# Product 3 of the first FFN's tiles a tile later, second buffers, and four banks for the transposes

## The chip, the cores and the metric

The kernel runs on one NeuronCore of a Trainium2 chip. The metric is the device time of one launch in microseconds (us). The engines have short names in the profile: PE is TensorE (matmuls and transposes; PEld its weight loads), DVE is VectorE, ACT is ScalarE, POOL is GpSimd, SP is SyncE, from whose queue most DMAs are issued. A lower time is better; the median of three runs is given, and one more execution was profiled.

## The reference

One layer of an encoder, applied with the same weights to a prompt of 1024 tokens and to a sample of 256 tokens, D = 1024, all in float32:

```
x <- LN1(alpha*x + 0.5*SwiGLU_1(x))
x <- LN2(alpha*x + W_out[ RMS(S5(x)) ; RMS(Hyena(x)) ])
x <- LN3(alpha*x + 0.5*SwiGLU_2(x))

_swiglu(x, w_gate, w_up, w_down) = (silu(x @ w_gate) * (x @ w_up)) @ w_down
```

The inner width of both FFNs is 2816, which is 22 tiles of 128. S5 is a bank of complex state space filters, Hyena a pair of long convolutions done with Fourier transforms. The change touches the first step of the prompt, above all; a detail of it touches the last.

## The kernel before

Float32 matmuls are made of three matmuls of a rounded format: each operand is split into a rounded part hi and a remainder lo, and hi times hi, hi times lo and lo times hi are added up in PSUM. `split` does this: ACT rounds (L171), DVE subtracts (L172).

The prompt's first FFN is done in two pieces. Two of its eight token tiles run with the sample's (`ffn`, L298 and L331 in the profile). The other six run in `ffn1_halves`: the token tiles are paired, and gate and up of a pair with the two halves of D are a product of 2 by 2 blocks, done with seven products instead of eight. `Blocks` makes the seven token operands: 11, 21 and 22 are blocks of the tokens, t1 to t4 their differences (on POOL, L1311). Each block of 128 by 512 is turned by four PE transposes into one PSUM bank (`Blocks.put`, L1318) and split from there. `GateUp` makes the seven weight operands of a tile of 128 inner columns: g1, g2 and u2 are blocks of the weights, s1 to s4 sums, which in the first FFN stand on POOL (L1373). Raw weights come by two DMAs of 512 KB per tile (L1345). The operand buffers of a weight are given back as soon as its product has been issued, so the next tile's split waits for that product on PE.

Product n of tile ft is written P(n, ft) below. Each is 12 matmuls of 128 by 384. Two sets of three PSUM banks alternate between tiles: bank a takes P1 and P2, bank b takes P6, P7 and P4, bank c takes P5 and P3, each adding on what is there. Between them the bank is read: after P1 a copy c1 (ACT), after P2 the first Silu (ACT L1437), after P6 the sum u2, after P7 two sums u3 (from b, then from c), after P4 the sum c1 and the product L1460, after P3 the sum, a second Silu (L1467) and the product L1468 (all sums are L1419 on DVE). The finished pair of h goes to DRAM by an SP DMA of 384 KB (L1488). After the last tile, `Down` reads it back and does the second matmul (L1552).

The order on PE in the loop of `gated` is: P1 of tile ft+1, P4 and P3 of ft, then P6, P5, P2 and P7 of ft+1. P4 has to wait until the first u3 sum has read bank b. u2 and u3 are the two halves of one buffer, and there is one buffer for h.

`weave` mixes two generators: while one issues the seven products, the other, `s5_mats`, prepares tables for S5 (cmul L424 to L429, L548 on DVE; a few matmuls; DMAs of scr_tab and scr_mat), by the shares that their yields name. The order of issue is turned into an order on each engine by a scheduler that goes by priority and estimated times.

Before the loop, `begin` issues the second pair of weight sums and the blocks 22 and t1 to t4 of all pairs (`Blocks.odd`). In the first FFN the transposes use banks 6 and 7 in turn, the last two that the products leave free.

The second FFN (prompt of eight token tiles, 128 by 512 matmuls) calls the same `gated`, with its weight sums on DVE, and with nothing woven in. Its first operands are made in `HyenaSide.prompt` while the mixer's last matmuls run, also through two banks.

Of the kernel before, what the change touches and what calls it, by code (L numbers as in the profile page):

```python
# [17 lines left out]
NFT = DFF // 128  # L18
# [10 lines left out]
PIECE = 2048  # L29
# [4 lines left out]
def prod(t):  # L34
    r = 1
    for v in t:
        r *= v
    return r


def shaped(ap, dims):
    if len(dims) == 1:
        return ap
    names = "abcde"[:len(dims)]
    return ap.rearrange("p (" + " ".join(names) + ") -> p " + " ".join(names), **dict(zip(names[1:], dims[1:])))
# [47 lines left out]
class Ring:  # L93
# [3 lines left out]
    def get(self):  # L97
        self.i += 1
        return self.bufs[(self.i - 1) % len(self.bufs)].v

    def free(self):
        for b in self.bufs:
            b.free()


class Banks:
# [436 lines left out]
def s5_mats(K, A, keep, scr, cfg):  # L543


    nc = K.nc
# [3 lines left out]
    turn, bs = K.new(7, 2, 32), K.new(2, 64, 16)  # L550
# [4 lines left out]
    for j in range(0, 32, 8):  # L555
        d, q = divmod(j, 16)
        c, s, t = c_.get(), s_.get(), tm.get()
        V.memset(c[:, :, 0:1], 1.0)
        V.memset(s[:, :, 0:1], 0.0)
        for lev in range(7):  # L560
            n = 1 << lev
# [16 lines left out]
    banks, bank1 = Banks(K, cfg["prep"][:-1]), Banks(K, cfg["prep"][-1:])  # L578
    bb, bb1 = bs.v[:, 0], bs.v[:, 1]
    pwr, pwi = K.pw[:, 0], K.pw[:, 1]  # L580
    cin, cst, gw = K.ring(2, 2, 2, 64), K.ring(1, 2, 8, 16), K.ring(2, 15, 16)
    inj, injt = K.ring(1, 4, 8, 16), K.ring(2, 4, 128)
    outm, tmp = K.ring(1, 4, 9, 16), K.ring(1, 4, 9, 16)
    nc.sync.dma_start(out=K.dcol, in_=g("ssm_d").rearrange("(b g) h -> (g h) b", b=4))
    for b in range(4):
        gv = gw.get()
# [58 lines left out]
        for s in range(8):  # L645
            nc.sync.dma_start(out=scr["mat"][s * 16:s * 16 + 16, b * 8:b * 8 + 8, 4].rearrange("h g x -> g h x"),
                              in_=gv[:, 7 - s:15 - s].rearrange("p t h -> p (t h)"))
    for r in (cin, cst, gw, inj, injt, outm, tmp, bs):
        r.free()


# [756 lines left out]
        self.w.pop(ft)  # L1408


def gated(K, X, G, hd, ids, begin, spare):

    nc = K.nc
    V = nc.vector
    T = X.width
    cr, tmp, hb = K.ring(2, T), K.new(2, T), K.ring(1, 2, T)
    TT = lambda o, a, b: V.tensor_tensor(out=o, in0=a, in1=b, op=ALU.add)  # L1419
    st = {}  # L1420
    END = NFT - 1

    def product(ft, n, bank, first):
        G.product(ft, n, X, st[ft]["ps"][bank], first)
        if ft == END:
            spare(n)

    def p1(ft):
        st[ft] = s = {"ps": [K.ps[:, b * 512:b * 512 + T] for b in ids[ft % 2]], "c1": cr.get()}
        product(ft, 1, 0, True)  # L1430
        nc.scalar.copy(out=s["c1"], in_=s["ps"][0])

    def p2(ft):
        s = st[ft]
        product(ft, 2, 0, False)
        s["h"] = hb.get()
        nc.scalar.activation(out=s["h"][:, 0], in_=s["ps"][0], func=AF.Silu)  # L1437

    def p6(ft):
        s = st[ft]  # L1440
        product(ft, 6, 1, True)
        s["u2"] = tmp.v[:, 0]
        TT(s["u2"], s["ps"][1], s["c1"])

    def p5(ft):
        product(ft, 5, 2, True)

    def p7(ft):
        s = st[ft]
        product(ft, 7, 1, False)  # L1450
        s["u3"] = tmp.v[:, 1]
        TT(s["u3"], s["ps"][1], s["c1"])
        TT(s["u3"], s["ps"][2], s["u3"])

    def p4(ft):
        s = st[ft]
        product(ft, 4, 1, False)
        h = s["h"][:, 0]
        TT(s["c1"], s["ps"][1], s["c1"])
        V.scalar_tensor_tensor(out=h, in0=s["c1"], scalar=0.5, in1=h, op0=ALU.mult, op1=ALU.mult)  # L1460

    def p3(ft):
        s = st[ft]
        product(ft, 3, 2, False)
        h = s["h"][:, 1]
        TT(h, s["ps"][2], s["u2"])
        nc.scalar.activation(out=h, in_=h, func=AF.Silu)  # L1467
        V.scalar_tensor_tensor(out=h, in0=s["u3"], scalar=0.5, in1=h, op0=ALU.mult, op1=ALU.mult)  # L1468

    p1(0)  # L1470
    p2(0)
    begin()
    G.parts(1)
    p1(1)
    p6(0)
    G.sums(1, 0)
    p5(0)
    G.sums(1, 1)
    p7(0)
    yield 0.6  # L1480
    for ft in range(NFT):
        if 0 < ft < END:
            p1(ft + 1)
        p4(ft)
        p3(ft)
        G.free(ft)
        G.load()
        nc.sync.dma_start(out=hd[ft], in_=st.pop(ft)["h"].rearrange("p a t -> p (a t)"))  # L1488
        yield 0.4
        if ft < END:  # L1490
            more = ft + 2 < NFT
            p6(ft + 1)
            if more:
                G.parts(ft + 2)
            p5(ft + 1)
            if more:
                G.sums(ft + 2, 0)
            p2(ft + 1)
            if more:
                G.sums(ft + 2, 1)  # L1500
            p7(ft + 1)
            yield 0.6
    for r in [cr, tmp, hb] + G.sv:
        r.free()


# [66 lines left out]
def run_all(gen):  # L1573
    for _ in gen:
        pass
# [18 lines left out]
def emit(ctx, tc, nc, A, dbg=None):  # L1594
# [34 lines left out]
    def tokens(ap, nm):  # L1629
        return ap.rearrange("(c s) d -> c s d", s=PARTS[nm][1])  # L1630
# [44 lines left out]

    def ffn1_halves(N, first, tail, turn):

        tb, src = Banks(K, (6, 7)), tokens(A["x_prompt"][0], "prompt")
        X = Blocks(K, N // 2, False)
        X.make(X.NAMES[0:2])  # L1680
        xs = [K.new(2, D) for _ in range(N // 2)]
        for j, x in enumerate(xs):
            for i in range(2):
                nc.sync.dma_start(out=x.v[:, i], in_=src[:, first + 2 * j + i])
            X.even(x.v, j, tb)
        G = GateUp(K, g("ffn1_w_gate"), g("ffn1_w_up"), True)
        G.load()
        yield 0.01
        G.parts(0)
        X.make(X.NAMES[2:])  # L1690
        G.load()

        def begin():
            G.sums(0, 0)
            G.sums(0, 1)
            for j, x in enumerate(xs):
                X.odd(x.v, j, tb)
                x.free()

        dn = Down(K, g("ffn1_w_down"), scr["h1"], N)  # L1700
        xr = []

        def spare(n):

            X.free(GateUp.OPS[n][1])
            if n in (1, 2):
                dn.load()
            elif n == 6:
                xr.append(Parts(K, N, D))
                for s in range(N):  # L1710
                    nc.sync.dma_start(out=xr[0].at(s), in_=src[:, first + s])

        yield from gated(K, X, G, scr["h1"], ((0, 1, 2), (3, 4, 5)), begin, spare)

        def done(s):
            nc.sync.dma_start(out=scr["x1_prompt"][:, first + s], in_=xr[0].at(s))
            turn(xr[0], s)

        yield from dn.run(xr[0], g("ln1_g"), g("ln1_b"), range(6), done, tail=tail)
        xr[0].free()  # L1720
# [65 lines left out]
    class HyenaSide:  # L1786


        def __init__(self, nm):
            self.nm, self.T = nm, NTOK[nm]  # L1790
            self.W = out_weights(K, A, 1)
# [37 lines left out]
        def prompt(self, ids, ids2, G):  # L1829


            tb = Banks(K, ids)
            self.norms(ids)
            lnb = self.norm_rows()
            x, nxt = {}, 0

            def load():
                nonlocal nxt
                x[nxt] = b = K.new(2, D)
                for i in range(2):  # L1840
                    nc.sync.dma_start(out=b.v[:, i], in_=scr["x1_prompt"][:, 2 * nxt + i])
                nxt += 1

            load()
            load()
            X = None

            def turn(j):
                X.even(x[j].v, j, tb)
                X.odd(x[j].v, j, tb)  # L1850
                x.pop(j).free()

            for j in range(4):
                for i in range(2):
                    s = 2 * j + i
                    for _ in mix_out(K, (s,), lambda s: x[j].v[:, i], self.hy, self.W, rs["prompt"][:, 1], ids2, lambda s: 0, 2):
                        pass
                    layer_norm(K, x[j].v[:, i], lnb.v[:, 0], lnb.v[:, 1], LN_EPS / ALPHA ** 2)
                    nc.sync.dma_start(out=scr["x2"][:, s], in_=x[j].v[:, i])
                    if i == 0 and j:  # L1860
                        if X is None:
                            X = Blocks(K, 4, True)
                            X.make(X.NAMES)
                        turn(j - 1)
                        if nxt < 4:
                            load()
                        elif j == 3:
                            G.load()
                free_all([self.hy[j]])
            free_all([self.W])  # L1870
            X.even(x[3].v, 3, tb)

            def begin():
                X.odd(x[3].v, 3, tb)
                x.pop(3).free()
                lnb.free()
                X.tmp.free()

            return X, begin
# [55 lines left out]
            for s in range(8):  # L1935
                nc.sync.dma_start(out=xr[0].at(s), in_=scr["x2"][:, s])

    run_all(gated(K, X, G, scr["h"], ((0, 1, 2), (3, 4, 5)), begin, spare))
    dst = tokens(A["out_prompt"], "prompt")

    def cut(c):
# [35 lines left out]
```

## Time and profile before

| what | us |
|---|---|
| median of three runs (lowest to highest) | 2590.32 (2585.53 to 2593.26) |
| the profiled execution | 2594.09 |
| its span, first to last instruction | 2592.3 |
| first FFN's products begin, six token tiles | 532.8 |
| first wait of the loop's P4 in PE's timeline | 571.7 |
| end of the first FFN's gate and up, about | 922 |
| second FFN's gate and up, about | 1915 to 2346 |
| its Down, to the end | 2346 to 2592 |

The mean granted clock of TensorE is 0.987 of the full one over the span. A row of a timeline has the start, the duration, the engine, the line, the operation, what is written from what (buffer numbers left out), shapes, a count of like instructions in a row, and in brackets the idle time of the engine ahead of it with what ended it. A row of the waits has the total, the number and the longest. A row of a window has the busy time of every engine, then PE's clock and the DMAs.

### The profile page before, as it was taken

How to read it: one execution, taken by the hardware profiler on the slowest of the kernel's cores; microseconds unless marked ns; L12 is line 12 of the kernel's file. 1: busy time of each engine (PE TensorE's matmuls, PEld its weight loads, DVE VectorE, ACT ScalarE, POOL GpSimd, SP SyncE). 2: the span in 40 equal slices, each digit the busy share in tenths (PEclk: the TensorE clock that was granted, in tenths of full speed). 3: DMA queues.
4: the chain of work that ended last, by engine and by line, in shares of the span. 5: the costliest groups of instructions: out<-in, count | busy, mean ns of one | idle time of the engine just before them, and what ended most of it. 6: DMA issues, size and time to landing. Idle time of an engine off the chain costs nothing.

```text
span 2592.3 us, 32411 instructions
## 1 busy us (share of the span) xinstructions
PE 2494.5 (96%) x12605; PEld 2123.9 (82%) x12605; DVE 1900.4 (73%) x2873; ACT 870.3 (34%) x1291; POOL 213.2 (8%) x158
## 2 busy tenths in 40 slices
PE   8999999988999999999999999999989999999998
PEld 6777777878899988888888878998768888888887
DVE  6887777697777886567896888788986656557437
ACT  5434443333333332223444313333332222223200
POOL 0000000143333300010000000000230000000001
PEclk9999999999999999999999999999989999999999
DMA  7333222434454564455565754565332322245311
GB/s 189 122 119 98 94 89 86 154 107 129 135 139 131 150 220 152 116 162 142 172 191 166 230 196 149 161 189 159 134 119 89 94 73 92 79 138 195 123 41 65
DMA packets 358704, 349.42 MB, mean 135 GB/s; under 512 B 41260, under 2 KB 308421, under 8 KB 357526
## 3 DMA queue, kind: packets, MB, share of 16 engines
q1 hardware_dynamic: 323510, 328.99, 40.5%
q10 hardware_dynamic: 35040, 18.35, 2.7%
q8 instruction: 99, 1.62, 0.3%
q14 instruction: 55, 0.45, 0.1%
HBM read 262.64 MB, written 84.39 MB: 134 GB/s over the span
## 4 chain that ended last, share of the span: by engine, by line
PE 69%; DVE 17%; DMA 5%; issue 3%; ACT 2%; POOL 2%; SPq 1%; ACTq 0%; DVEq 0%; POOLq 0%
PE banks L1398 24%; PE banks L1552 14%; PE banks L298 9%; PE banks L331 5%; DVE s L172 4%; PE banks L866 3%; DVE s L936 3%; PE banks L783 3%; PE banks L1248 2%; PE banks L1070 2%; ACT s L171 2%; POOL s L1373 1%; DVE s L751 1%; DMA s<-in_ffn_w_up_dram 1%; DMA s<-in_ffn_w_gate_dram 1%
## 5 line engine op out<-in xcount | busy, mean ns | idle before, releaser
L1398 PE MATMUL banks<-s,s 128*128 128x512 f32 (+1 forms) x3536 | 767.5, 369 | 19.4 <-DVE s L1419 15.6
L171 ACT ACTIVATE s<-s 128x1024 fp32r<-128x1024 f32 (+4 forms) x533 | 481.0, 916 | 855.6 <-PE banks L1398 176.0
L1398 PEld LDWEIGHTS banks<-s,s 128*128 128x128 f32 x3536 | 651.7, 191 | 97.6 <-DVE s L1419 15.6
L172 DVE TENSOR_TENSOR s<-s,s 128x1024 fp32r<-128x1024 f32 (+4 forms) x533 | 575.1, 1089 | 198.6 <-ACT s L171 187.0
L298 PE MATMUL banks<-s,s 128*128 128x512 f32 (+1 forms) x2112 | 400.9, 342 | 2.6 <-ACT s L171 1.7
L1552 PE MATMUL banks<-s,s 128*128 128x512 f32 x1232 | 386.8, 394 | 0.0
L298 PEld LDWEIGHTS banks<-s,s 128*128 128x128 f32 x2112 | 324.8, 191 | 53.6 <-issue 9.2
L1552 PEld LDWEIGHTS banks<-s,s 128*128 128x128 f32 x1232 | 230.4, 188 | 47.8 <-DVE s L172 0.4
L1552 PE MATMUL banks<-s 128*128 128x512 f32 x616 | 242.4, 394 | 0.0
L1419 DVE TENSOR_TENSOR s<-banks,s 128x384 f32<-128x384 f32 (+1 forms) x220 | 136.6, 621 | 139.0 <-PE banks L1398 137.5
L866 PE MATMUL banks<-s,s 128*128 128x512 f32 (+1 forms) x1152 | 237.6, 360 | 0.0
L866 PEld LDWEIGHTS banks<-s,s 128*128 128x128 f32 x1152 | 188.0, 189 | 28.0 <-DVE s L172 0.4
L331 PE MATMUL banks<-s,s 128*128 128x512 f32 x792 | 199.7, 398 | 3.0 <-DVE s L172 1.1
L1558 DVE TENSOR_TENSOR s<-banks,s 128x512 f32<-128x512 f32 x140 | 96.1, 688 | 129.4 <-PE banks L1552 129.4
L230 POOL TENSOR_TENSOR cst<-cst 128x1 f32<-128x1 f32 (+2 forms) x38 | 47.8, 1259 | 1619.5 <-DVE cst L229 1619.5
L331 PEld LDWEIGHTS banks<-s,s 128*128 128x128 f32 x792 | 146.7, 190 | 35.2 <-issue 1.9
L1552 PEld LDWEIGHTS banks<-s 128*128 128x128 f32 x616 | 115.8, 188 | 24.1
L1248 PE MATMUL banks<-s,s 128*128 128x512 f32 x480 | 124.3, 406 | 3.8 <-DVE s L1170 1.6
L1248 PEld LDWEIGHTS banks<-s,s 128*128 128x128 f32 x480 | 89.3, 191 | 23.4 <-DVE s L1170 2.0
L685 DVE TENSOR_TENSOR s<-banks,s 128x512 f32<-128x512 f32 (+2 forms) x112 | 58.8, 551 | 41.7 <-ACT s L802 20.8
L783 PEld LDWEIGHTS banks<-s,s 128*128 128x128 f32 x624 | 81.0, 190 | 7.1 <-ACT s L171 2.5
L783 PE MATMUL banks<-s,s 128*128 128x256 f32 x624 | 85.8, 285 | 0.0
(217 smaller groups left out, 2531.7 us busy)
## 6 DMA issues: line engine op xcount, KB each, us to landing
s<-in_ffn_w_gate_dram SPq DMA_DIRECT2D x88, 512.0 KB
s<-in_ffn_w_up_dram SPq DMA_DIRECT2D x88, 512.0 KB
s<-in_ffn_w_down_dram SPq DMA_DIRECT2D x88, 512.0 KB
scr_h<-s SPq DMA_DIRECT2D x22, 512.0 KB
s<-scr_h SPq DMA_DIRECT2D x22, 512.0 KB
scr_tab<-s ACTq DMA_DIRECT2D x32, 320.0 KB
s<-scr_mat SPq DMA_DIRECT2D x16, 640.0 KB
s<-scr_tab SPq DMA_DIRECT2D x16, 640.0 KB
```

What stands on the lines that cost most here:

```text
L171: K.nc.scalar.activation(out=hi, in_=src, func=AF.Copy)
L172: K.nc.vector.tensor_tensor(out=lo, in0=src, in1=hi.bitcast(F32), op=ALU.subtract)
L298: nc.tensor.matmul(pss[-1][c], lhsT=w[:, wv, d], rhs=xT.parts[k][c].at(d), start=(d == 0 and wv == 0 and k == 0), stop=(d == 7 and wv == 1))
L331: nc.tensor.matmul(ps, lhsT=h[s // 4][:, a, s % 4 * 128:(s % 4 + 1) * 128], rhs=w[:, b, dh * 512:(dh + 1) * 512], start=(n == 0), stop=(n ...
L783: nc.tensor.matmul(ps, lhsT=F[kt][a].v[:, s, i], rhs=b.v[:, s], start=(n == 0), stop=(n == 3 * NT // R - 1))
L866: nc.tensor.matmul(p, lhsT=w[:, wv, d], rhs=xT[nm].parts[k][c].at(d), start=(d == 0 and wv == 0 and k == 0), stop=(d == 7 and wv == 1))
L936: TT = lambda o, a, b, op: V.tensor_tensor(out=o, in0=a, in1=b, op=op)
L1248: nc.tensor.matmul(ps, lhsT=y[s // per][a].v[:, k, ts], rhs=W[k].v[:, b, dh * 512:dh * 512 + 512], start=(k == 0 and a == 0 and b == 0), s ...
L1398: self.K.nc.tensor.matmul(ps, lhsT=w[i][:, d], rhs=x[k][:, d], start=first and m == 0, stop=m == len(todo) - 1, skip_group_check=True)
L1419: TT = lambda o, a, b: V.tensor_tensor(out=o, in0=a, in1=b, op=ALU.add)
L1552: nc.tensor.matmul(ps, lhsT=p[a].v[:, o:o + 128], rhs=p[b].v[:, dh * 512:dh * 512 + 512], start=m == 0, stop=m == len(todo) - 1)
L1558: nc.vector.tensor_tensor(out=xv, in0=ps, in1=xv, op=ALU.add)
```

## The change

`gated` gets an argument `late`. Where it is true (first FFN), P3 of a tile is issued after P7 of the next one instead of behind P4 of its own; u2, u3 and h have two buffers each; the write of h to DRAM goes with P3; and the raw weights of a further tile are requested once a tile's sums are issued, after two more in `begin`, which puts them a tile further ahead. Where it is false (second FFN) the order of products stays. The transposes in `ffn1_halves` go through banks 4, 5, 6 and 7; those of the second FFN's operands through 2, 3 and two more, and in its `begin` through 4 to 7. The small rings of the S5 preparation are packed into two pieces of SBUF, and the buffers of `gated` are taken when first used.

The counts of instructions on PE, DVE, ACT and POOL stay the same.

```diff
+class Later(Ring):
+    def __init__(self, K, n, *dims):
+        super().__init__([])
+        self.K, self.n, self.dims = K, n, dims
+    def get(self):
+        if len(self.bufs) < self.n:
+            self.bufs.append(self.K.new(*self.dims))
+            self.i = len(self.bufs) - 1
+        return super().get()
...
-    cin, cst, gw = K.ring(2, 2, 2, 64), K.ring(1, 2, 8, 16), K.ring(2, 15, 16)
-    inj, injt = K.ring(1, 4, 8, 16), K.ring(2, 4, 128)
-    outm, tmp = K.ring(1, 4, 9, 16), K.ring(1, 4, 9, 16)
+    inj, injt, cin, whole1 = packed(K, (1, 4, 8, 16), (2, 4, 128), (2, 2, 2, 64))
+    outm, tmp, cst, gw, whole2 = packed(K, (1, 4, 9, 16), (1, 4, 9, 16), (1, 2, 8, 16), (2, 15, 16))
...
-def gated(K, X, G, hd, ids, begin, spare):
+def gated(K, X, G, hd, ids, begin, spare, late):
...
-    cr, tmp, hb = K.ring(2, T), K.new(2, T), K.ring(1, 2, T)
+    rings = cr, u2r, u3r, hb = [Later(K, n, *d) for n, *d in ((2, T), (1 + late, T), (1 + late, T), (1 + late, 2, T))]
...
         V.scalar_tensor_tensor(out=h, in0=s["u3"], scalar=0.5, in1=h, op0=ALU.mult, op1=ALU.mult)
+        G.free(ft)
+        nc.sync.dma_start(out=hd[ft], in_=st.pop(ft)["h"].rearrange("p a t -> p (a t)"))
+
+    def weights(ft, step):
+        if ft < NFT:
+            (G.parts, lambda f: G.sums(f, 0), lambda f: G.sums(f, 1))[step](ft)
+            if step == 2 and late:
+                G.load()
...
-    yield 0.6
+    yield 0.7
     for ft in range(NFT):
+        if ft and late:
+            p3(ft - 1)
         if 0 < ft < END:
             p1(ft + 1)
         p4(ft)
-        p3(ft)
-        G.free(ft)
-        G.load()
-        nc.sync.dma_start(out=hd[ft], in_=st.pop(ft)["h"].rearrange("p a t -> p (a t)"))
+        if not late:
+            p3(ft)
+            G.load()
         yield 0.4
         if ft < END:
...
             p6(ft + 1)
-            if more:
-                G.parts(ft + 2)
+            weights(ft + 2, 0)
             p5(ft + 1)
...
+            weights(ft + 2, 1)
             p2(ft + 1)
...
+            weights(ft + 2, 2)
             p7(ft + 1)
...
+    if late:
+        p3(END)
...
-        tb, src = Banks(K, (6, 7)), tokens(A["x_prompt"][0], "prompt")
+        tb, src = Banks(K, (4, 5, 6, 7)), tokens(A["x_prompt"][0], "prompt")
...
-        G.load()
 
         def begin():
             G.sums(0, 0)
             G.sums(0, 1)
+            G.load()
+            G.load()
...
-            tb = Banks(K, ids)
+            tb, tb2 = Banks(K, (2, 3) + ids), Banks(K, ids2 + ids)
...
-                X.odd(x[3].v, 3, tb)
+                X.odd(x[3].v, 3, tb2)
```

What this does to the engines shows in the middle of the first FFN's loop. First PE, where P7 of tile 9 ends (weights s_60 and s_61). Before, P1 of tile 10 (weights s_45 and s_46) follows, and after that P4 of tile 9:

```order
L1398 MATMUL banks<-s_61_3649,s_86_4913 128x384
L1398 MATMUL banks<-s_60_3648,s_86_4913 128x384
L1398 MATMUL banks<-s_45_3447 128x384
L1398 MATMUL banks<-s_46_3448,s_45_3447 128x384
L1398 MATMUL banks<-s_45_3447,s_46_3448 128x384
```

Now P3 of tile 8 (weights s_54 and s_55) stands there, with P1 of tile 10 and P4 of tile 9 behind it (L1426 is the L1398 of before):

```order
L1426 MATMUL banks<-s_61_3649,s_82_4749 128x384
L1426 MATMUL banks<-s_60_3648,s_82_4749 128x384
L1426 MATMUL banks<-s_54_3642,s_56_3644 128x384
L1426 MATMUL banks<-s_55_3643,s_56_3644 128x384
L1426 MATMUL banks<-s_54_3642,s_57_3645 128x384
```

Twelve matmuls more stand between P7 and P4 of one tile. Next DVE at the same place, before: the first u3 sum of tile 9, two splits of tile 10 (L172), the second u3 sum and the c1 sum (the row with x2), L1460, and then the sum and the product behind P3 of tile 9:

```order
L1419 TENSOR_TENSOR s_65_3655<-banks,s_65_3655 128x384
L172 TENSOR_TENSOR s_55_3643<-s_65_3655,s_54_3642 128x512
L172 TENSOR_TENSOR s_88_5042<-s_66_3656,s_88_5042 128x512
L1419 TENSOR_TENSOR s_65_3655<-banks,s_65_3655 128x384 x2
L1460 SCALAR_TENSOR_TENSOR s_66_3656<-s_65_3655,s_66_3656 128x384
L1419 TENSOR_TENSOR s_66_3656<-banks,s_65_3655 128x384
L1468 SCALAR_TENSOR_TENSOR s_66_3656<-s_65_3655,s_66_3656 128x384
```

After the change DVE has, behind the two u3 sums of tile 9, the sum and the product of P3 of tile 8 (L1447 and L1496), and then the c1 sum and L1488 (L1460 before) of tile 9:

```order
L1447 TENSOR_TENSOR s_71_3877<-banks,s_64_3652 128x384
L201 TENSOR_TENSOR s_61_3649<-s_64_3652,s_60_3648 128x512
L201 TENSOR_TENSOR s_85_5012<-s_65_3679,s_85_5012 128x512
L1447 TENSOR_TENSOR s_71_3877<-banks,s_71_3877 128x384
L1447 TENSOR_TENSOR s_64_3652<-banks,s_65_3679 128x384
L1496 SCALAR_TENSOR_TENSOR s_64_3652<-s_65_3679,s_64_3652 128x384
L1447 TENSOR_TENSOR s_64_3652<-banks,s_64_3652 128x384
L1488 SCALAR_TENSOR_TENSOR s_72_3878<-s_64_3652,s_72_3878 128x384
```

The first u3 sum keeps its place against the splits; the P3 sum has come forward past the c1 sum, and it belongs to the tile before. Last SP, where writes of h (scr_h) and raw weight loads alternate, before:

```order
L1488 DMA scr_h_73<-s_66_3656 128x768
L1345 DMA s_97_5651<-in_ffn_w_gate_dram 128x8x128
L1345 DMA s_97_5651<-in_ffn_w_up_dram 128x8x128
L1488 DMA scr_h_73<-s_66_3656 128x768
L1345 DMA s_101_5796<-in_ffn_w_gate_dram 128x8x128
L1345 DMA s_101_5796<-in_ffn_w_up_dram 128x8x128
L1488 DMA scr_h_73<-s_66_3656 128x768
```

After, in the middle of the loop:

```order
L1373 DMA s_90_5434<-in_ffn_w_gate_dram 128x8x128
L1373 DMA s_90_5434<-in_ffn_w_up_dram 128x8x128
L1498 DMA scr_h_73<-s_64_3652 128x768
L1498 DMA scr_h_73<-s_72_3878 128x768
L1373 DMA s_92_5563<-in_ffn_w_gate_dram 128x8x128
L1373 DMA s_92_5563<-in_ffn_w_up_dram 128x8x128
```

Two writes of h, of two tiles and from two buffers, now stand next to each other between pairs of loads.

More of the change, by code (lines that the diff above doesn't have):

```diff
@@ L103, in free, with __init__, packed @@
             b.free()
+class Later(Ring):
[7 more added lines that the diff above has]
+        return super().get()
+class Slice:
+    def __init__(self, v):
+        self.v = v
+def packed(K, *rings):
+    whole, o, out = K.new(PIECE), 0, []
+    for n, *dims in rings:
+        m = prod(dims)
+        out.append(Ring([Slice(shaped(whole.v[:, o + i * m:o + i * m + m], dims)) for i in range(n)]))
+        o += n * m
+    return *out, whole
 class Banks:
@@ L647, in s5_mats @@
                               in_=gv[:, 7 - s:15 - s].rearrange("p t h -> p (t h)"))
-    for r in (cin, cst, gw, inj, injt, outm, tmp, bs):
+    for r in (whole1, whole2, bs):
         r.free()
@@ L1441, in p6 @@
         product(ft, 6, 1, True)
-        s["u2"] = tmp.v[:, 0]
+        s["u2"] = u2r.get()
         TT(s["u2"], s["ps"][1], s["c1"])
@@ L1450, in p7 @@
         product(ft, 7, 1, False)
-        s["u3"] = tmp.v[:, 1]
+        s["u3"] = u3r.get()
         TT(s["u3"], s["ps"][1], s["c1"])
@@ L1477, in gated @@
     p5(0)
-    G.sums(1, 1)
+    weights(1, 2)
     p7(0)
-    yield 0.6
+    yield 0.7
     for ft in range(NFT):
+        if ft and late:
+            p3(ft - 1)
         if 0 < ft < END:
@@ L1484, in gated @@
         p4(ft)
-        p3(ft)
-        G.free(ft)
-        G.load()
-        nc.sync.dma_start(out=hd[ft], in_=st.pop(ft)["h"].rearrange("p a t -> p (a t)"))
+        if not late:
+            p3(ft)
+            G.load()
         yield 0.4
         if ft < END:
-            more = ft + 2 < NFT
             p6(ft + 1)
-            if more:
-                G.parts(ft + 2)
+            weights(ft + 2, 0)
             p5(ft + 1)
-            if more:
-                G.sums(ft + 2, 0)
+            weights(ft + 2, 1)
             p2(ft + 1)
-            if more:
-                G.sums(ft + 2, 1)
+            weights(ft + 2, 2)
             p7(ft + 1)
             yield 0.6
-    for r in [cr, tmp, hb] + G.sv:
+    if late:
+        p3(END)
+    for r in rings + G.sv:
         r.free()
@@ L1711, in spare @@
                     nc.sync.dma_start(out=xr[0].at(s), in_=src[:, first + s])
-        yield from gated(K, X, G, scr["h1"], ((0, 1, 2), (3, 4, 5)), begin, spare)
+        yield from gated(K, X, G, scr["h1"], ((0, 1, 2), (3, 4, 5)), begin, spare, True)
         def done(s):
@@ L1936, in spare @@
                 nc.sync.dma_start(out=xr[0].at(s), in_=scr["x2"][:, s])
-    run_all(gated(K, X, G, scr["h"], ((0, 1, 2), (3, 4, 5)), begin, spare))
+    run_all(gated(K, X, G, scr["h"], ((0, 1, 2), (3, 4, 5)), begin, spare, False))
     dst = tokens(A["out_prompt"], "prompt")
```

## The prediction

> **What bounds the kernel now.** I read the page's first lines, then the windows view over the stretches that the change touches, then the waits in them, and last the timelines of single engines.
>
> ```profile
> PE 2494.5 (96%) x12605; PEld 2123.9 (82%) x12605; DVE 1900.4 (73%) x2873; ACT 870.3 (34%) x1291; POOL 213.2 (8%) x158
> 500.00:560.00 60.00, 47.57 (x235) 39.18 (x233) 50.77 (x82) 19.07 (x35) 30.30 (x22) 0.91 0.32 105
> 560.00:760.00 200.00, 178.89 (x958) 175.66 (x959) 157.37 (x327) 70.88 (x128) 67.73 (x48) 0.94 0.44 124
> 760.00:922.00 162.00, 155.78 (x918) 152.34 (x916) 122.20 (x182) 64.13 (x127) 48.63 (x35) 1.00 0.53 152
> 1900.00:1934.00 34.00, 26.35 (x117) 19.89 (x114) 30.50 (x39) 14.54 (x23) 15.58 (x11) 0.80 0.29 94
> 2000.00:2040.00 40.00, 40.00 (x178) 33.11 (x178) 22.70 (x30) 10.86 (x15) 0.00 (x0) 1.00 0.26 79
> ```
>
> The columns of a window are its length, then busy time and count of PE, PEld, DVE, ACT and POOL, then PE's granted clock, the DMA share and GB/s. PE is the bound: 96% over the span, and in the second FFN's gate/up (2000 to 2040) it has no gap at all. The program order that `gated` writes for that FFN stays as it is, so the change can earn there only where the stage begins. In the first FFN's gate/up, 560 to 922, PE lacks 21.1 us before 760 and 6.2 us after it, 27.3 in all, and before 760 its clock was granted at 0.94, worth about 0.06 x 200 = 12 us. These 39 us are all that this stage can give; its matmuls are the same before and after. The waits say who holds PE (waiter, releaser: us in total, times, longest):
>
> ```profile
> PE banks L1398 <- DVE s L1419: 27.3, 16, 3.2
> POOL s L1373 <- DVE s L172: 181.6, 35, 12.1
> ACT s L171 <- POOL s L1373: 100.4, 52, 4.5
> ACT s L1437 <- DMA scr_h<-s: 8.6, 5, 3.0
> ```
>
> One wait makes up the whole gap: a product waits for L1419, the sum out of PSUM. Eleven of the 16 stand in PE's timeline (start, duration, count, then the idle time ahead):
>
> ```profile
> 571.72 2.32 PE L1398 MATMUL banks<-s,s 128*128 128x384 f32 x12 [2.13 <-DVE s L1419]
> 580.40 4.43 PE L1398 MATMUL banks<-s,s 128*128 128x384 f32 x24 [0.99 <-DVE s L1419]
> 588.74 10.67 PE L1398 MATMUL banks<-s,s 128*128 128x384 f32 x60 [1.83 <-DVE s L1419]
> 603.65 14.31 PE L1398 MATMUL banks<-s,s 128*128 128x384 f32 x72 [2.15 <-DVE s L1419]
> 637.26 3.13 PE L1398 MATMUL banks<-s,s 128*128 128x384 f32 x12 [2.65 <-DVE s L1419]
> 654.89 0.44 PE L1398 MATMUL banks<-s 128*128 128x384 f32 x1 [1.18 <-DVE s L1419]
> 687.29 0.69 PE L1398 MATMUL banks<-s 128*128 128x384 f32 x1 [2.98 <-DVE s L1419]
> 706.71 14.33 PE L1398 MATMUL banks<-s,s 128*128 128x384 f32 x72 [1.85 <-DVE s L1419]
> 739.82 3.26 PE L1398 MATMUL banks<-s,s 128*128 128x384 f32 x12 [2.14 <-DVE s L1419]
> 759.48 0.44 PE L1398 MATMUL banks<-s 128*128 128x384 f32 x1 [3.22 <-DVE s L1419]
> 790.20 0.44 PE L1398 MATMUL banks<-s 128*128 128x384 f32 x1 [1.30 <-DVE s L1419]
> ```
>
> The waiting product is 4, which writes bank b again after 7, as soon as the first of the two sums behind product 7 has read it. What makes that sum late is seen at the longest stall:
>
> ```profile
> 745.35 8.83 PE L1398 MATMUL banks<-s,s 128*128 128x384 f32 x50
> 751.74 2.81 POOL L1373 TENSOR_TENSOR s<-s,s 128x512 f32<-128x512 f32 x1 [11.13 <-DVE s L172]
> 754.58 0.63 ACT L171 ACTIVATE s<-s 128x512 fp32r<-128x512 f32 x1 [4.01 <-POOL s L1373]
> 755.25 3.11 DVE L172 TENSOR_TENSOR s<-s,s 128x512 fp32r<-128x512 f32 x2 [1.85 <-ACT s L171]
> 758.88 0.55 DVE L1419 TENSOR_TENSOR s<-banks,s 128x384 f32<-128x384 f32 x1
> ```
>
> GpSimd makes a weight sum for the next tile, ACT rounds it, DVE forms the rest (L172), and only then, in DVE's order, comes the sum that PE needs. PE was out of work at 756.2 and went on at 759.48.
>
> **Product 3 as cover.** Before, one product (1 of the next tile) stood between 7 and 4; after, there are two, 3 of the tile before and 1. A product is 12 matmuls of 8.83 / 50 = 0.177 us, so 2.1 us of cover. Taking up to 2.1 off each of the eleven stalls removes 2.1 + 0.99 + 1.83 + 2.1 + 2.1 + 1.18 + 2.1 + 1.85 + 2.1 + 2.1 + 1.3 = 19.7 of their 22.4 us. The other five of the 16 hold 27.3 - 22.4 = 4.9 us; counted as no longer than 2.1 each, they go. That is 24.6, which is the upper bound if DVE's queue stays as early as it is against PE. It won't wholly: DVE's work doesn't shrink.
>
> ```profile
> 560.00:922.00 362.00, 334.67 (x1874) 328.00 (x1874) 279.57 (x508) 135.01 (x255) 116.36 (x82) 0.97 0.48 137
> ```
>
> DVE is busy 279.6 of 362 us (77%). In a stage of about 335 us it would be 83%, with the bursts of S5 preparation still between the splits. I give back 4.6 us for that and **take 20**; the lower bound is 9, where DVE delays keep two thirds of the waits.
>
> **The clock.** The clock sags where the stalls are long (0.94 to 760) and not where they are short (1.00 after 760, with one stall of 1.30). By my count nothing over 1.2 us is left. Of the 12 us some belongs to the gaps of the stage's beginning, which stay in part. **I take 7**; bounds 0 and 12.
>
> [...]
>
> ```profile
> 580.00:600.00 20.00, 17.77 (x101) 17.48 (x102) 14.78 (x24) 7.33 (x13) 7.94 (x6) 1.00 0.43 123
> ...
> 660.00:680.00 20.00, 20.00 (x118) 20.00 (x117) 11.09 (x30) 6.53 (x12) 5.55 (x4) 1.00 0.62 177
> 680.00:700.00 20.00, 17.02 (x82) 16.70 (x82) 18.95 (x46) 6.30 (x12) 5.74 (x4) 0.83 0.25 73
> ```
>
> The clock was 1.00 in the 20 us without a gap and 0.83 in the 20 us with this stall; the shorter stalls of 580 to 600 cost none.
>
> **Buffers and DMAs that the move needs.** Second buffers of u2, u3 and h let product 6, 2 and 7 of the next tile write before product 3 of this one has been read; that costs SBUF, no instruction. Product 5 of the next tile now waits for L1419 behind 3 (same bank c). Between 3 and that 5 stand products 1, 4 and 6, 6.3 us of PE; the sum takes 0.55 us (row of 758.88) plus DVE's queue, which at the longest stall was 758.88 - 756.2 = 2.7 us late. So about 3 us are to spare: nothing, with 0 to 3 us over the stage as bounds. The write of h (SP, L1488) goes out a tile later. Before, its buffer was wanted by ACT's L1437 after three products; with two buffers it is wanted after five (1, 4, 6, 5, 2), 10.5 us minus 0.55 for each of three operations in between, about 8.8 us.
>
> ```profile
> 748.27 0.33 SPq L1488 DMA_DIRECT2D scr_h<-s  x1
> 755.12 0.48 ACT L1437 ACTIVATE s<-banks 128x384 f32<-128x384 f32 x1
> ```
>
> Here 6.9 us were enough without a wait. The five waits of 8.6 us in all go; ACT is no bound, so I count nothing (bounds 0 and 2). Weight loads are issued one tile earlier. They never show among the long waits now, so nothing again.
>
> **Four banks for the transposes, first FFN.** Before the stage runs smoothly PE transposes operands through two banks and waits for the lo split to free one:
>
> ```profile
> PE banks L1318 <- DVE s L172: 7.0, 5, 3.1
> 540.42 0.63 PE L1318 MATMUL banks<-cst,s 128*128 128x128 f32 x4 [1.67 <-DVE s L172]
> 544.15 1.09 PE L1318 MATMUL banks<-cst,s 128*128 128x128 f32 x4 [3.11 <-DVE s L172]
> ```
>
> (The first row is the waits view of 534 to 562.) Four banks let PE run ahead, but each block still needs its difference on GpSimd and its two splits, and DVE is busy 50.8 of these 60 us. Bounds 0 and 8, counting the waits and some clock (0.91); **I take 3**.
>
> **Four banks, second FFN.** The same two rows of thought, with a different releaser:
>
> ```profile
> 1909.15 1.29 DVE L245 SCALAR_TENSOR_TENSOR s<-s,cst,s 128x1024 f32<-128x1024 f32 x1 [2.42 <-POOL cst L230]
> 1911.18 1.68 PE L1318 MATMUL banks<-cst,s 128*128 128x128 f32 x8 [3.21 <-DVE s L172]
> ```
>
> The split that PE waits for stands on DVE behind a layer norm that waits for GpSimd, and the last token tile comes from that norm. Banks don't make it come earlier. Nothing; bounds -2 (a loss) and 6, since PE lacks 7.7 us of 34 there. The packing of the S5 scratch changes addresses alone.
>
> **The sum.** -20 - 7 - 3 = -30 us. The profiled execution took 2594.1 us (its span is 2592.3), 3.8 more than the median of the three runs, 2590.3. Minus 30 that is 2564, or 2560 by the median. I forecast 2562.
>
> **The rivals.**
>
> *The clock does not come back.* The low clock of 560 to 760 comes from something other than product 4's stalls (the stage's beginning, or the S5 work that is denser there) and stays. Then -20 - 3 = -23 us, 2571 from the profiled time and 2567 from the median: 2569. Against it stand the two windows above; for it, that the clock was 1.00 in the window of 580 to 600 in spite of the stalls at 580.40 and 588.74. Chance 0.15. [...]
>
> *DVE and GpSimd become the bound.* The chain of the longest stall has its time in GpSimd and in DVE operations that took longer than usual:
>
> ```profile
> L172 DVE TENSOR_TENSOR s<-s,s 128x512 fp32r<-128x512 f32 x143 | 116.8, 826 | 40.3 <-ACT s L171 34.7 <-PE banks L632 4.2
> L1419 DVE TENSOR_TENSOR s<-banks,s 128x384 f32<-128x384 f32 x106 | 58.5, 551 | 29.8 <-PE banks L1398 29.1
> L1373 POOL TENSOR_TENSOR s<-s,s 128x512 f32<-128x512 f32 x41 | 58.4, 1425 | 204.0 <-DVE s L172 160.7 <-DVE s L558 10.7 <-DVE s L428 8.0
> ```
>
> The pair of splits at 755.25 took 3.11 us where two mean ones take 1.65, and GpSimd's sum at 751.74 took 2.81 where the mean is 1.43: they stretch where they meet. All of GpSimd's 116.4 us and DVE's work outside L1419, 279.6 - 58.5 = 221.1, make 337 us if none of it may overlap. The stage would stop near 345 instead of 335: -17 with the clock's part included, and with nothing at the beginning, about 2574. Chance 0.13. [...]
>
> *The wait only moves.* Product 5 or 7 waits for the same late DVE, because every sum in the tile is later by what 4 was. Then 27.3 us stay and the time is 2588 to 2594, no change. Against it: DVE has 23% free and the stalls are single events, not one per tile. Chance 0.09.
>
> *Slower: the SP queue.* Writes of h now stand on SP behind a pair of weight loads of a deeper prefetch, and these wait until GpSimd's second pair of sums gives a raw buffer back. If this holds a write of h back by more than 8.8 - 6.9 = 1.9 us in most tiles, L1437 waits, and behind it on ACT all roundings, behind these DVE's splits. At 3 us in each of 20 tiles it costs 60 us, less the 30 gained: about 2620. It decides from 1.5 us per tile on. For it: POOL's waits for DVE reach 12.1 us. Chance 0.06.
>
> **How the numbers follow.** The forecast has 0.52; a larger gain (the upper bounds of the stalls, the clock and the beginning, -24.6 - 12 - 4 = about -41, 2550) 0.05; then 0.15, 0.13, 0.09 and 0.06. The range reaches from 2548 (upper bounds) to 2588 and leaves out the slower case and most of no change. About 0.3% (8 us) is what a measurement of this kernel can tell from no change, so faster begins below 2582.5. Faster: 0.52 + 0.05 + 0.15 + 0.11 of the third = 0.83; same: 0.09 + 0.02 = 0.11; slower: 0.06.
>
> **What would show it.** In the changed profile, waits of L1398 products for the sum out of PSUM, from 545 to the end of the stage, should be under 10 us instead of 27.3, and the clock of the first 200 us at 0.97 or more. The stage should last about 335 us. Longer waits with product 5 as waiter, or of ACT's first Silu for the write of h, would show the third and fourth rival; clock windows below 0.95 without stalls the first; DVE over 85% busy with PE still waiting the second. I am wrong if the stage isn't shorter by 15 us.

## The result and the profile after

The changed kernel takes 2572.96 us (median of five runs, 2568.30 to 2577.55) against 2590.32 us (five runs, 2585.53 to 2601.58): a ratio of 0.9926, with a 95% interval of 0.9898 to 0.9955. That is 17.4 us faster, where 28 were forecast. The profiled execution has a span of 2573.4 us, 18.9 under that of before. The windows view of both kernels, cut at the same two events (the wait of product 4 of the first tile, the first matmul of Down), shows where. Of before:

```profile
571.70:921.40 349.70, 324.48 (x1821) 318.34 (x1822) 268.81 (x482) 130.64 (x246) 113.20 (x80) 0.97 0.48 138
921.40:1128.10 206.70, 205.58 (x996) 170.15 (x995) 152.73 (x204) 53.22 (x66) 5.12 (x4) 1.00 0.50 158
1128.10:1835.50 707.40, 685.71 (x3918) 599.16 (x3917) 565.04 (x810) 260.80 (x440) 12.19 (x9) 1.00 0.57 174
```

Of after:

```profile
559.10:906.30 347.20, 329.00 (x1857) 322.33 (x1858) 283.27 (x503) 128.31 (x246) 114.73 (x80) 0.98 0.48 140
906.30:1108.20 201.90, 200.47 (x963) 164.84 (x963) 148.83 (x197) 53.04 (x68) 7.54 (x5) 1.00 0.51 162
1108.20:1816.70 708.50, 687.85 (x3917) 600.60 (x3916) 564.69 (x809) 260.51 (x440) 10.70 (x8) 1.00 0.57 173
```

The loop is 2.5 us shorter and Down with what follows 4.8. Both belong together: 36 PE instructions more now lie in the loop and 33 fewer behind it. Of the 36, 28 are matmuls of the products themselves, mostly because before the change PE does 24 of the last ones behind Down's first matmul, and 8 are S5's. So loop and Down gave 7.3 us. The mixers are as long as before (+1.1), and so is all behind them: 2592.3 - 1835.5 = 756.8 us before, 2573.4 - 1816.7 = 756.7 after.

The stretch ahead of the loop is 571.7 - 559.1 = 12.6 us shorter, but not all of that is the change's. The first product of this FFN starts at 532.8 us before and at 525.5 after, and in the profiles of the experiments below anywhere from 523 to 533, though the program of the first 500 us is the same. Before's profile has a clock of 0.97 from 0 to 100 us and 0.98 from 400 to 500 us where after's has 1.00, which is about 5 us of that difference. A measure that this scatter doesn't touch is the time from the FFN's first product to its last: 396.6 us before (to 929.4) and 381.1 after (to 906.6). That is 15.5 us, about 2.5 of them for 11 matmuls of Down that stand among the last products of before.

The waits of after, first for the loop, and PE's longest stall with what stood on DVE and GpSimd ahead of it:

```profile
PE banks L1426 <- DVE s L1447: 15.0, 11, 3.1
```

```profile
690.68 5.81 PE L1426 MATMUL banks<-s,s 128*128 128x384 f32 x17 [3.14 <-DVE s L1447]
```

```profile
681.66 0.69 DVE L453 TENSOR_TENSOR s<-s,s 128x512 f32<-128x512 f32 x1
682.27 0.42 DVE L458 TENSOR_TENSOR s<-s,s 128x256 f32<-128x256 f32 x1
682.60 0.69 DVE L201 TENSOR_TENSOR s<-s,s 128x512 fp32r<-128x512 f32 x1
683.20 0.69 DVE L454 TENSOR_TENSOR s<-s,s 128x512 f32<-128x512 f32 x1
683.80 1.78 DVE L456 TENSOR_TENSOR s<-s,s 128x512 f32<-128x512 f32 x1
685.51 1.78 DVE L455 TENSOR_TENSOR s<-s 128x512 f32<-128x512 f32 x1
687.21 1.28 DVE L201 TENSOR_TENSOR s<-s,s 128x512 fp32r<-128x512 f32 x2
688.41 1.75 DVE L457 TENSOR_TENSOR s<-s,s 128x512 f32<-128x512 f32 x1
690.08 0.55 DVE L1447 TENSOR_TENSOR s<-banks,s 128x384 f32<-128x384 f32 x1
```

```profile
683.43 1.60 POOL L1401 TENSOR_TENSOR s<-s,s 128x512 f32<-128x512 f32 x1 [10.89 <-DVE s L201]
685.12 1.62 POOL L1401 TENSOR_TENSOR s<-s 128x512 f32<-128x512 f32 x1
687.97 1.64 POOL L1401 TENSOR_TENSOR s<-s 128x512 f32<-128x512 f32 x1 [1.23 <-DVE s L201]
```

(In after's numbering L1401 are the weight sums, L1447 the sums out of PSUM, L201 the splits, L453 to L458 the S5 tables.) PE ended product 1 at 687.5 and stood until the sum at 690.08. DVE has no gap here: six table operations and three splits are ahead of the sum. Three of the table operations took 1.75 to 1.78 us, where the same shape takes 0.69 at 683.20, and all three ran while GpSimd made its sums. Counting twelve matmuls a product in PE's timeline, product 4 now waits 8 times for 12.5 us in all (13 times and 22.4 us before), and product 7, behind the sum of product 6, 4 times for 3.3 us (once for 1.0, which is the row of 580.40 in the prediction).

### The profile page after: what moved, and what is told of

Read it like the earlier page. It is cut to its first block, busy times and chain, and to the rows that moved or that the text cites. A ratio compares the mean times of both kernels' runs of the same rounds, so it can differ in the third digit from the quotient of the medians.

```text
span 2573.4 us, 32411 instructions
## 1 busy us (share of the span) xinstructions
PE 2487.4 (97%) x12605; PEld 2117.4 (82%) x12605; DVE 1904.3 (74%) x2873; ACT 865.8 (34%) x1291; POOL 216.8 (8%) x158
## 4 chain that ended last, share of the span: by engine, by line
PE 68%; DVE 19%; DMA 4%; issue 3%; POOL 3%; ACT 3%; SPq 0%; ACTq 0%; DVEq 0%; POOLq 0%
PE banks L1426 21%; PE banks L1587 14%; PE banks L327 9%; PE banks L360 5%; PE banks L894 4%; DVE s L201 4%; DVE s L964 3%; PE banks L1276 3%; PE banks L811 3%; PE banks L1098 2%; ACT s L200 2%; POOL s L1401 2%; DVE s L779 1%; POOL s L1339 1%; DVE s L1012 1%
## 5 line engine op out<-in xcount | busy, mean ns | idle before, releaser
L1426 PE MATMUL banks<-s,s 128*128 128x512 f32 (+1 forms) x3544 | 762.7, 368 | 18.2 <-DVE s L1447 11.5
L1426 PEld LDWEIGHTS banks<-s,s 128*128 128x128 f32 x3544 | 650.4, 190 | 97.3 <-DVE s L1447 14.8
L201 DVE TENSOR_TENSOR s<-s,s 128x1024 fp32r<-128x1024 f32 (+4 forms) x533 | 567.1, 1076 | 182.2 <-ACT s L200 174.5
L1447 DVE TENSOR_TENSOR s<-banks,s 128x384 f32<-128x384 f32 (+1 forms) x220 | 135.8, 620 | 123.5 <-PE banks L1426 122.5
```

The source lines that it names most:

```text
L201: K.nc.vector.tensor_tensor(out=lo, in0=src, in1=hi.bitcast(F32), op=ALU.subtract)
L1426: self.K.nc.tensor.matmul(ps, lhsT=w[i][:, d], rhs=x[k][:, d], start=first and m == 0, stop=m == len(todo) - 1, skip_group_check=True)
```

## The experiments

Each kernel is timed against the kernel before on the same chip. The theories were, at first: the gain of the beginning is the banks' (A); the stalls that are left come from DVE's table work (C) or from the chain GpSimd, ACT, DVE that makes the next weights (D).

**e1_banks**, the kernel before with the first FFN's four banks alone:

```diff
-        tb, src = Banks(K, (6, 7)), tokens(A["x_prompt"][0], "prompt")
+        tb, src = Banks(K, (4, 5, 6, 7)), tokens(A["x_prompt"][0], "prompt")
```

> The kernel before with one edit: the first FFN's transposes take banks 4 to 7. Theory A (the beginning's gain of about 8 us comes from the banks alone): the stretch from 483 us to the first FFN's second tile is 6 to 8 us shorter than before, the loop's waits of products for the sum out of PSUM stay near 27 us, the time falls by 6 to 8 us. Theory B (the beginning gained because products or loads were put in another order): the beginning gains under 3 us and the time is within 3 us of before.

2585.82 us against 2588.45, a ratio of 0.9984 (0.9972 to 0.9996): 3 to 4 us. Neither expectation is met well; the banks are worth about 3 us, less than A says, and the loop's waits stay (29.6 us in 16).

**e2_late**, the changed kernel with both bank edits undone:

```diff
-        tb, src = Banks(K, (4, 5, 6, 7)), tokens(A["x_prompt"][0], "prompt")
+        tb, src = Banks(K, (6, 7)), tokens(A["x_prompt"][0], "prompt")
...
-            tb, tb2 = Banks(K, (2, 3) + ids), Banks(K, ids2 + ids)
+            tb = tb2 = Banks(K, ids)
```

> The changed kernel with both bank edits undone: product 3 late, second buffers and the further loads alone. Theory A: the beginning is as before (within 2 us), the loop's waits for sums fall from 27 to about 15 us, and the time is 8 to 12 us below before. Theory B: the whole gain of about 17 us is there without the banks.

2575.37 us, 0.9949 (0.9931 to 0.9966), so 13 us without the banks, between the two expectations and nearer to A's. The waits for sums are 14.5 us in 12. With e1 the parts add up to the whole: 0.9984 x 0.9949 = 0.9933. From the FFN's first product to its last, e1 takes 394.3 us and e2 378.0, near before (396.6) and after (381.1). So the late product 3 shortens the stage, together with the second buffers and the further loads that came with it; no run takes these apart.

**e5_notab** and **e6_notab_before**, the changed kernel and the one before without the two largest levels of the S5 tables. Those entries stay zero, so both kernels leave out a part of S5:

```diff
             n = 1 << lev
-            cmul(K, c[:, :, n:2 * n], s[:, :, n:2 * n], c[:, :, 0:n], s[:, :, 0:n],
+            if n < 32:
+                cmul(K, c[:, :, n:2 * n], s[:, :, n:2 * n], c[:, :, 0:n], s[:, :, 0:n],
...
```

> The changed kernel without the two largest levels of the S5 tables (their powers from 32 on stay zero, 12 DVE operations in each of 4 tables, about 26 us of DVE work; PE's work stays). Theory C (the stalls left after the change come from DVE, whose queue holds the tables' large operations ahead of the sums): the waits of products for sums fall from 15 us to under 5, the clock from 560 us to 760 us is 0.98 or more, and the stage is 10 us shorter than the changed kernel's 347. Theory D (the chain GpSimd, ACT, DVE that makes the next tile's weights sets them): the waits stay at 10 us or more.

> The kernel before without the same two levels. Theory C with one product of cover being too little even without them: waits for sums 8 to 15 us, the time 8 to 15 us under before. If the tables made all the stalls: under 4 us, and product 3's place is worth nothing without them. Theory D: waits stay near 27 us.

2554.62 us, 0.9867 (0.9848 to 0.9887), and 2579.32 us, 0.9966 (0.9950 to 0.9983). The waits of e5_notab and of e6_notab_before for the sums out of PSUM, one row each:

```profile
PE banks L1429 <- DVE s L1450: 5.7, 9, 2.1
```

```profile
PE banks L1401 <- DVE s L1422: 17.1, 14, 3.1
```

C holds in the changed kernel: without 26 us of table work the waits fall to 5.7, near the under 5 that was expected. In the kernel before they stay at 17.1, between the 8 to 15 of C's second case and the 27 of D: there one product of cover is too little even without the tables. Without that work the whole change is worth 2579.3 - 2554.6 = 25 us, with it 17. The windows of 560 to 760 us of before, after and e5_notab, in this order, show the clock beside the stalls:

```profile
560.00:760.00 200.00, 178.89 (x958) 175.66 (x959) 157.37 (x327) 70.88 (x128) 67.73 (x48) 0.94 0.44 124
```

```profile
560.00:760.00 200.00, 185.28 (x1011) 181.79 (x1010) 163.92 (x338) 73.53 (x134) 70.89 (x49) 0.96 0.48 132
```

```profile
560.00:760.00 200.00, 197.65 (x1132) 195.33 (x1132) 153.60 (x308) 81.17 (x151) 72.39 (x55) 1.00 0.53 144
```

PE has 958, 1011 and 1132 matmuls done in the same 200 us, at 0.94, 0.96 and 1.00 of its clock. The clock follows the sum of the waits only loosely: e2_late, with 14.5 us of waits against after's 15.0, had 0.99 in this stretch.

**e7_spread** and **e8_spread_before** spread the table work (the largest level in two halves, yields by size), in the changed kernel and in the one before:

```diff
...
-            yield 1.5
...
+                yield {1: 0.5, 2: 0.5, 4: 0.5, 8: 0.5, 16: 1.0, 32: 2.5, 64: 5.0}[n] * m / 8
```

> The changed kernel with the S5 tables' work spread: the largest level in two halves, and the yields by the size of a level (0.5 to 5) instead of 1.5 each; the same sums are computed, with 24 more DVE operations. Theory E (what stalls PE is the burst, several large table operations in a row ahead of a sum): the waits for sums fall from 15 to under 9 us, and the time is 4 to 10 us below the changed kernel. Theory F (it is DVE's load as a whole, so it doesn't matter how the work lies): waits stay within 3 us of 15, the time within 4 us.

> The same spreading in the kernel before. Since without the tables' large levels 19 of the 22 us of product 4's stalls were still there, the tables are not what stalls it: waits of product 4 stay at 18 to 25 us and the time within 5 us of before. If spreading is worth as much here, it is 8 us or more faster.

2577.25 us, 0.9947 (0.9932 to 0.9962), and 2590.92 us, 1.0011 (0.9996 to 1.0026): nothing gained. The changed kernel still has 13.6 us of stalls ahead of product 4, and the kernel before 25.8. But this doesn't decide between E and F: in the traces the table work still comes in four bursts, as in the changed kernel, with about 10 us or more almost without any between them.

**e10_half** makes the tables in eight halves with two buffers, so that the next one needn't wait until the last is written out:

```diff
-    c_, s_, n_, tm = (K.ring(1, 8, n) for n in (160, 160, 160, 64))
-    for j in range(0, 32, 8):
+    c_, s_, n_, tm = (K.ring(r, 4, n) for r, n in ((2, 160), (2, 160), (2, 160), (1, 64)))
+    for j in range(0, 32, 4):
...
```

> The changed kernel with the S5 tables made in eight halves of four groups with two buffers each, in place of four tables with one buffer (same SBUF, about 170 DVE operations more of 0.1 to 0.7 us, half the size each, twice as many writes of scr_tab). Theory G (the tables come in bursts because the next one waits until the last has been written out, 10 to 20 us without table work and then 30 us in which DVE is full): the work lies evenly, waits for sums fall from 15 to under 9 us and the time is 4 to 8 us below the changed kernel. If DVE's sum of work is what counts: waits stay or grow, and the time is the same or up to 6 us longer.

2580.80 us, 0.9962 (0.9948 to 0.9977), 8 us slower than the changed kernel, with 20.2 us of stalls ahead of product 4. Here the table work does lie more evenly, almost without such gaps, but it has grown from 78 to 100 us, and DVE's busy time over the loop's products from 288.0 to 308.0. The waits grew with the sum of work; whether an even layout of the same work would help isn't shown.

**e3_first** gives the first sum behind product 7 a higher priority:

```diff
-        TT(s["u3"], s["ps"][1], s["c1"])
+        with K.tc.high_priority(offset=60):
+            TT(s["u3"], s["ps"][1], s["c1"])
```

> The changed kernel with a higher priority (by 60) for the first sum behind product 7: on DVE it moves ahead of one or two of the weight splits, the table work stays ahead of it. If the splits ahead of the sum (0.7 us each) matter: 0.7 to 1.3 us off each of the 8 stalls of product 4, 6 to 10 us in all. If the tables alone matter: stalls of product 4 stay at 10 us or more and the time is within 4 us of the changed kernel.

2572.48 us, 0.9934 (0.9912 to 0.9957): as the changed kernel. Product 4 still stalls 8 times, for 11.4 us. The run says little about the splits, since the edit hardly changed DVE's order: the sum passed one split in 2 of 21 tiles.

**e9_pool** puts half of the large table operations on GpSimd:

```diff
+    if t2 is not None:
+        V, t = K.nc.gpsimd, t2
     V.tensor_tensor(out=outi, in0=ar, in1=bi, op=ALU.mult)
...
```

> The changed kernel with three of the six operations of the two largest table levels on GpSimd instead of DVE, with a scratch buffer of their own (about 13 us of DVE work less, 24 operations of some 0.8 to 1.6 us more on GpSimd). If DVE's own queue is what counts: waits for sums fall to 7 to 11 us and the time by 5 to 8 us. If GpSimd and DVE hold each other up (operations that stretched from 0.68 to 1.78 us beside GpSimd's sums), or GpSimd's sums come late behind the new work, the waits stay or rise, and the time is the same or up to 10 us longer.

2575.44 us, 0.9949 (0.9931 to 0.9968), not faster. DVE gave away 24 operations, yet its busy time over the loop's products stayed (288.4 us from 552.3 to 901.3 us, 288.0 from 554.6 to 906.6 in the changed kernel). So I turned to what GpSimd costs DVE. In the changed kernel's loop 53 DVE operations that ran beside a GpSimd one took 50 us more than the shortest of their own line and shape. The 37 sums with an operand in PSUM that ran beside one took at most 0.02 us more.

**e11_dvesums** moves the weight sums from GpSimd to DVE:

```diff
-        eng = K.nc.gpsimd if self.fine else K.nc.vector
+        eng = K.nc.vector
```

> The changed kernel with the weight sums of the first FFN on DVE instead of GpSimd: 79 operations of 0.68 us, 54 us, come to DVE in the stage, and the about 49 us by which DVE's operations beside GpSimd's are stretched in the changed kernel's trace go. Theory H (GpSimd and DVE exclude each other, so GpSimd's sums take DVE's time anyway): DVE's busy time in the stage grows by less than 15 us from 283, the waits for sums stay between 8 and 20 us and the time is within 5 us of the changed kernel. If the sums on GpSimd are really beside DVE's work: DVE's busy time grows by 40 us or more, PE waits 25 us or more and the time is over 10 us longer.

2555.66 us, 0.9861 (0.9842 to 0.9881): 35 us under the kernel before and 17 under the changed one, the best version of the study. H was right about DVE's time, but its 8 to 20 us of waits and unchanged time did not come: of the waits for sums 1.6 us are left. The groups of DVE by shape in the loop, a row of the loop's waits and its window, of after:

```profile
L201 DVE TENSOR_TENSOR s<-s,s 128x512 fp32r<-128x512 f32 x140 | 107.7, 784 | 27.5 <-ACT s L200 26.6
L1447 DVE TENSOR_TENSOR s<-banks,s 128x384 f32<-128x384 f32 x108 | 58.9, 551 | 16.8 <-PE banks L1426 16.5
```

```profile
ACT s L200 <- POOL s L1401: 98.7, 47, 5.8
559.00:907.00 348.00, 329.70 (x1861) 322.94 (x1862) 284.07 (x506) 128.90 (x246) 114.83 (x80) 0.98 0.48 140
```

And of e11_dvesums, with the row of the waits for sums:

```profile
L201 DVE TENSOR_TENSOR s<-s,s 128x512 fp32r<-128x512 f32 x144 | 96.7, 685 | 7.2 <-ACT s L200 7.0
L1447 DVE TENSOR_TENSOR s<-banks,s 128x384 f32<-128x384 f32 x108 | 59.6, 553 | 27.3 <-PE banks L1426 27.1
L1401 DVE TENSOR_TENSOR s<-s,s 128x512 f32<-128x512 f32 x41 | 28.1, 686 | 0.2
L1401 DVE TENSOR_TENSOR s<-s 128x512 f32<-128x512 f32 x41 | 28.1, 685 | 0.1
```

```profile
PE banks L1426 <- DVE s L1447: 1.6, 1, 1.6
555.00:887.00 332.00, 324.71 (x1881) 320.73 (x1881) 284.65 (x609) 131.58 (x252) 0.00 (x0) 0.99 0.50 147
```

DVE took over 82 operations of 56 us, and its busy time is the same: 284.1 us before the move, 284.7 after it. The splits fell from 784 to 685 ns. L1447, which reads one operand from PSUM, is at 551 and 553 ns, with GpSimd or without. From the first product to the last the FFN takes 358.7 us (381.1 in the changed kernel).

**e12_dvesums_before** is the kernel before with the same line changed.

> The kernel before with one edit, the weight sums of the first FFN on DVE. Theory I (GpSimd's sums are what made DVE late in both kernels; with them gone one product of cover does): the time falls by 25 us or more, to about 2560, and product 3's place is worth under 8 us on top. Theory J (the cover is needed as well): product 4 still stalls by 10 us or more in all, the time falls by 8 to 20 us, and the changed kernel with sums on DVE (2556) stays 12 us or more ahead.

2566.40 us (2557.29 to 2568.45), 0.9903 (0.9879 to 0.9927). In the profile, which is of the fastest of the four (2557.29), 3.3 us are left of the stalls ahead of product 4. That is nearer to I: with the sums on DVE one product of cover nearly does. By the medians the whole change (banks, product 3, buffers, loads) is worth 2566.4 - 2555.7 = 11 us on top, but e12's four runs lie 11 us apart, and the fastest of them is within 2 us of e11's median. How much of it is product 3's isn't settled.

**e13_both** leaves the sums on DVE and lets GpSimd make four sums per tile that nobody reads:

```diff
...
+            for v in (x, y):
+                K.nc.gpsimd.tensor_tensor(out=self.idle.v, in0=u[:, 0:4], in1=v, op=ALU.add)
```

> The changed kernel with the sums on DVE, and with GpSimd making four sums of the same shapes per tile as well, into a buffer that nobody reads. Theory K (GpSimd and DVE shut each other out, so it is GpSimd's running at all that cost the time): DVE's splits (128 by 512) go up from a mean of 685 ns to 780 or more, waits for sums and weights to 10 us or more, the time to 2568 or more. Theory L (what cost the time was that the next tile's weights came by way of GpSimd, whose sums take twice as long and stand two engines before DVE's splits): the time stays within 6 us of 2556.

2619.14 us, 1.0107 (1.0083 to 1.0131): 63 us slower than e11, through work whose results nothing reads. Its DVE groups, two rows of its waits and its window:

```profile
L201 DVE TENSOR_TENSOR s<-s,s 128x512 fp32r<-128x512 f32 x144 | 114.1, 806 | 1.0 <-ACT s L200 0.7
L1452 DVE TENSOR_TENSOR s<-banks,s 128x384 f32<-128x384 f32 x106 | 58.0, 549 | 27.3 <-PE banks L1431 27.2
```

```profile
PE banks L1431 <- DVE s L1452: 25.5, 13, 4.0
PE banks L1346 <- POOL s L1339: 9.6, 4, 4.9
575.00:955.00 380.00, 338.77 (x1886) 329.82 (x1885) 343.08 (x610) 131.81 (x252) 117.77 (x72) 0.97 0.43 128
```

48 of the 63 us lie in the window (380 us, 332 in e11). Some 16 lie between the FFN's first product and the window: there GpSimd still makes the differences of the tokens (L1339), the sums that nobody reads stand ahead of them, and PE's transposes wait 9.6 us for GpSimd. In the window DVE is busy 343 instead of 285 us with the same operations, and that is 90% of it. K's numbers came: beside GpSimd's sums the splits, whose operands lie in SBUF, took 806 ns instead of 685, and nothing in the loop waits for what GpSimd makes, only for the raw buffers that it reads (ACT waits 4.3 us for raw weights). The sums with a PSUM operand did not stretch: 549 ns here, 553 in e11.

What e13 doesn't show is how the 17 us between the changed kernel and e11 come about. DVE's busy time is the same in these two, so they are no sum of DVE's time. Two things differ in when that time falls: single operations take 1.75 us instead of 0.69 just ahead of a sum that PE needs, and the next tile's weights come by way of GpSimd, for whose sums ACT waits 98.7 us in the changed kernel's loop (the way that L means). No run separates the two.

## Why the prediction came out as it did

- **Direction and mechanism: right.** With product 3 as a second product of cover, the stalls of product 4 fell from 22.4 to 12.5 us; e2_late shows that this comes without the banks. In the pair without the S5 tables' large levels the whole change is worth 25 us, nearer to the 30 forecast.
- **The stalls: the term that was mis-sized.** Forecast -20. Over all products they fell from 27.3 to 18.0 us (15.0 for the sums, 3.0 put down to other lines of DVE), -9. The step that failed is "I give back 4.6 us for that": I took DVE's 77% as slack that shrinks evenly, and so gave back 4.6 us where some 15 were needed. In the table bursts DVE is full (681 to 691 above), part of it stretched beside GpSimd, so the sums there are later against PE the sooner PE gets to them. e5_notab shows the tables' part (waits of 5.7 us), e11 that of GpSimd's sums (1.6 us).
- **The clock: mis-sized with the stalls.** Forecast -7. From 0.94 to 0.96 of 200 us is about -4, and over loop and Down together PE's busy time fell by only 0.6 us (530.1 to 529.5); some long stalls were left, such as the one of 3.14 us, in whose 20 us (680 to 700 of after) the clock was 0.83. The rival in which the clock doesn't come back fell: e11, with all of the S5 work and 1.6 us of waits for sums, has 0.99. In before the 20 us that had 0.83 are those with the stall of 2.98 us at 687.29.
- **The beginning: about right.** -3 forecast, 2.6 measured in e1_banks between medians, 4 by the ratio.
- **What I cost at nothing was nothing:** no product 5 waits for its bank in the changed kernel, ACT's first Silu waits 3.6 us for a write of h instead of 8.6, and the second FFN's banks gave 0.1 us. The rival of the SP queue and that of a wait that only moves did not happen, though a small new wait (product 7, 3.3 us) did.
- **The signs that I named did not come.** The waits are 15.0 us, not under 10, and the clock is 0.96, not 0.97. I wrote that I am wrong if the stage isn't shorter by 15 us: by the loop with Down it is 7.3 us shorter, and from first product to last 15.5, or 13 without Down's matmuls, the beginning's 3 included. So the stage gave much less than the 27 expected of it. The time lies inside the range because the range was wide, from 2548 to 2588.
- **The rival of DVE and GpSimd** was the nearest in its cause, and I gave it 0.13. That its 2574 meets the measured 2573 is luck in good part. Its 345 us were for a stretch that took 362 before; the loop that took 347 had taken 350. DVE is busy 82% of that loop, not the 85% that I named as the rival's sign. And the 337 us are no bound: that none of the two engines' work may overlap is shown by no run (in e13, GpSimd's sums of 117.8 us made DVE's busy time 58 us longer), and they add GpSimd's time to DVE rows that already hold what those were stretched beside GpSimd. In e11 DVE does the work of both in 284.7 us, in a loop of 332.

## What to carry to other kernels

In the changed kernel's loop DVE's busy time held 50 us by which its operations beside GpSimd's took longer than the shortest of their kind. A row of DVE that takes a multiple of its usual time while GpSimd is busy was the sign (1.78 us against 0.69), and moving GpSimd's sums to DVE left DVE's busy time as it was (284.1 and 284.7 us). Cover on PE for a late engine is worth only what that engine's queue leaves: read its lateness in the stretches where it is full, not from its share of the whole stage. Test a suspected contention by adding work that nobody needs to the engine as well as by taking its work away, and look whether anything else stands behind the added work in that engine's queue.

## What the runs showed of the hardware that was not expected

A GpSimd sum (1.6 us mean, 72 of them, 118 us) whose result nobody uses raised DVE's busy time in the stage from 285 to 343 us, about 0.8 us for each. TensorE's granted clock was lower around some stalls of before: 0.91 over 20 us (600 to 620) with one of 2.15 us, 0.83 over 20 us (680 to 700) around one of 2.98 us, 1.00 over 20 us (580 to 600) with stalls of 0.99 and 1.83. The length alone didn't decide it: the longest stall of before, 3.22 us, ended at 759.48, and the clock from 760 to 780 was 1.00.
